# Two chained nets on one core: the passage between them by token halves

## The chip, the core and the metric

The kernel runs on one core of a Trainium2 chip. The core has five engines with queues of their own: TensorE (PE in the profile, its weight loads PEld), VectorE (DVE), ScalarE (ACT), GpSimd (POOL) and SyncE (SP), from whose queue most transfers are issued. The metric is the device time of one execution in microseconds.

## The reference, cut to what matters

Input x has 512 tokens of 1024 channels. The first net has two layers (attention mixers and a gated feed-forward net); behind them stands an RMS norm with gain `g_final`. Its result goes into the second net, again two layers. What lies around the passage is this:

```
# end of the first net, layer 1
x = x + (silu(h @ w1) * (h @ w3)) @ w2
x = rms_norm(x, g_final)
# start of the second net, layer 0
shift, scale, gate = split(c @ w_ada + b_ada, 3)
h = layer_norm(x) * (1 + scale) + shift
proj = h @ w_in        # q, k, v, gates, convolution, Fourier part
...
x = layer_norm(ALPHA * x + (1 + gate) * y) * ln_g + ln_b
```

## The kernel before, in words

Activations lie transposed: a tile is 128 channels by 512 tokens, and x is eight such tiles. Matrix products are done as three products each of a high and a low part (lines 269 to 271, `mm3`); weights are loaded by `weights` (L263), and split into `whi` on ScalarE (L251) and `wlo` on VectorE (L252). There are two staging buffers `wst` and three pairs `whi`, `wlo`. PSUM has eight banks: three with the tag "mm", two "S", two "T", one "O"; a tag that doesn't exist, such as "ms", takes a "T".

**The last products of the first net.** The loop over n in `first_layer` makes one output tile per round: 22 steps of three products over `gh`, `gl` with the `w2` weights in three parts of 8, 8 and 6 steps. The function `f` in `build` (L1647) adds the residual `xo`, and `centre` follows: it squares the tile, forms `d = g * x - shift` (L1134, the tile `u`), squares that, and sends `d` by two transfers (L1137) to `hl[:, n]` and to `xd`. For tiles 1 to 6 GpSimd adds the three tiles to running sums. At n = 6 three products with a matrix of ones (`add_sum`, L1114) put those running sums into three banks; at n = 7 three more add the last tile, the modulation's gate is folded (L1103), and mean and scale of the norms are worked out on ScalarE and VectorE for all 512 tokens, with a root (L1185) and a reciprocal (L1194).

**The modulated input.** `less_mean` subtracts the mean (L1201 for tiles 3, 5, 7 on GpSimd, L1205 for the others on VectorE), and `put_h` makes the product with the scale (L1275), the high part `hh` on ScalarE (L1276) and the low part `hl` on VectorE (L1279). The subtractions on VectorE are let go one by one with `issue_after`, and the products use the tile tag `tmp` with four buffers. After that stands the reciprocal for `r0` (L1234).

**The value products.** `second_layer` first makes values and the Fourier input: four weight chunks `wvf2`, each for two tiles k of h, against four token tiles of 128: for each chunk, each k and each token tile three products of 384 columns. The splits of chunks 2 and 3 are put behind the third tile's product and high part (`self.behind`). Then come the key projection (24 products of 512 columns, tile `mm<-hh,whi`) and the rest of the layer.

**What sets the order.** The kernel is written as one program; a planner (`TileContext` with a simulated time line) orders each engine's queue: at every moment it gives the engine, of the instructions that are ready by its own estimates, the one that stands first in the program. `issue_after` adds an order on one engine and nothing else. Semaphores are put in by the planner. The tile pools are a stack: the feed-forward pools `ft1` and `fg1` (with `gh` and `gl`) are closed at the end of the first net, and the second net's pools `t2` and `c2` are opened in their memory; `xt`, the tiles with the mean taken off, are the first of `t2`.

Of the kernel before, what the change touches and what calls it, by code (L numbers as in the profile page):

```python
# [11 lines left out]
F32 = mybir.dt.float32  # L12
# [7 lines left out]
D = 1024  # L20
# [11 lines left out]
COFF = (0, -8, -16)  # L32
RPW = 64

GATES = (1, 0, 6, 1, 1, 4, 3)
W1 = 1.0
PAUSE = (12000, 9000)
# [177 lines left out]
class _Net:  # L215
# [357 lines left out]
    def first_layer(self, l, acc, xsrc, emit_x):  # L573
# [121 lines left out]
        with ExitStack() as fctx:  # L695
            self.tp = fctx.enter_context(self.tc.tile_pool(name=f"ft{l}", bufs=4))
            gp = fctx.enter_context(self.tc.tile_pool(name=f"fg{l}", bufs=1))
            r = gp.tile([P, S], F32, name=f"rf{l}")
            gh = gp.tile([P, NF, S], F32R, name=f"gh{l}")
            gl = gp.tile([P, NF, S], F32R, name=f"gl{l}")  # L700
            h = (self.hh, self.hl)
            extra = self.modulation() if l == DEPTH - 1 else iter(())
            for i in range(NF):
                for _ in range(3):
                    next(extra, None)
                pa, pb = self.any_bank(), self.any_bank()
                self.dense(pa, self.weights(a["w1"][l, i]), h, range(8))
                if i == 0:
                    self.inv_root(self.ones_sum(acc2), D, self.eps, r)
                self.dense(pb, self.weights(a["w3"][l, i]), h, range(8))  # L710
                u = self.t(self.tp, "u", (P, S), bufs=2)
                nc.vector.tensor_tensor(u, pa, r, op=ALU.mult)
                s = self.t(self.tp, "s", (P, S), bufs=2)
                nc.scalar.activation(s, u, AF.Silu)  # L714
                nc.gpsimd.tensor_tensor(s, s, r, op=ALU.mult)  # L715
                nc.vector.tensor_tensor(u, pb, s, op=ALU.mult)
                self.split(gh[:, i], gl[:, i], u)
            for n in range(8):
                ps = self.any_bank()
                for c0 in range(0, NF, 8):  # L720
                    c1 = min(c0 + 8, NF)
                    self.dense(ps, self.weights(a["w2"][l, n][:, c0 * P:c1 * P]), (gh, gl), range(c0, c1),
                               first=c0 == 0, last=c1 == NF)
                xo = self.t(self.tp, "xo", (P, S), bufs=2)
                nc.sync.dma_start(out=xo, in_=self.xd[2 * l][n])
                emit_x(n, ps, xo)
# [389 lines left out]
    def centre(self, n, x, state):  # L1116

        nc = self.nc
        g = self.col("g_final", n)
        if n == 0:  # L1120
            z = self.t(self.tp, "tmp", (P, S))
            nc.scalar.activation(z, x, AF.Copy, scale=g)
            pz = self.bank("ms")
            self.add_sum(pz, z, True, True)
            self.shift = self.fp.tile([P, S], F32, name="shift", tag="accf")
            nc.scalar.activation(self.shift, pz, AF.Copy, scale=1.0 / P)
            state["d"], state["x"] = (self.t(self.tp, "mw", (P, S), bufs=2) for _ in range(2))
            state["q"] = self.t(self.tp, "q", (P, S), bufs=1)
            d, sq, dq = state["d"], state["x"], state["q"]
        else:  # L1130
            d = self.t(self.tp, "u", (P, S), bufs=2)
            sq, dq = (self.t(self.tp, "tmp", (P, S)) for _ in range(2))
        nc.scalar.activation(sq, x, AF.Square)
        nc.vector.scalar_tensor_tensor(d, x, g, self.shift, op0=ALU.mult, op1=ALU.subtract)  # L1134
        nc.scalar.activation(dq, d, AF.Square)
        for dst in (self.hl[:, n].bitcast(F32), self.xd[0][n]):
            nc.sync.dma_start(out=dst, in_=d)  # L1137
        if 0 < n < 7:
            for k, y in (("d", d), ("x", sq), ("q", dq)):
                nc.gpsimd.tensor_tensor(state[k], state[k], y, op=ALU.add)  # L1140
        if n == 6:
            self.pm, self.pv, self.px = (self.bank(t) for t in "SOT")
            self.add_sum(self.px, state["x"], True, False)
            self.add_sum(self.pm, state["d"], True, False)
            self.add_sum(self.pv, state["q"], True, False)
            self.root_table(sq)
        if n == 7:
            self.add_sum(self.px, sq, False, True)
            self.add_sum(self.pm, d, False, True)
            at = self.add_sum(self.pv, dq, False, True)  # L1150
            pg = self.bank("mm")
            with self.tc.issue_after(at.ins):
                self.fold(pg, [self.gate_acc])

            self.mean = self.fp.tile([P, S], F32, name="mean", tag="accf")
            m2, q = (self.t(self.tp, t, (P, S), bufs=2) for t in ("s", "xo"))
            r = self.scale = self.fp.tile([P, S], F32, name="scale")
            nc.scalar.activation(m2, self.pm, AF.Square, scale=1.0 / D)
            nc.scalar.activation(self.mean, self.pm, AF.Copy, scale=1.0 / D)
            nc.vector.tensor_scalar(q, self.px, 1.0 / D, EPS, op0=ALU.mult, op1=ALU.add)  # L1160
            nc.vector.scalar_tensor_tensor(m2, q, LN_EPS, m2, op0=ALU.mult, op1=ALU.subtract)
            self.root_of(r, self.pv, m2, ALU.add, 0.0)
            self.one_over(r, r)
            with self.tc.issue_after(self.r_at):
                self.put_mod(0, pg, 2, 1)

    def root_table(self, x):

# [25 lines left out]
        self.r_at = self.nc.vector.reciprocal(r, v).ins  # L1194
        return r

    def less_mean(self, out, x, m, use):

        nc, late = self.nc, self.tc.issue_after
        for n in (3, 5, 7):  # L1200
            nc.gpsimd.tensor_tensor(out[n], x[n], m, op=ALU.subtract)  # L1201

        def sub(n, at):
            with late(at):
                nc.vector.tensor_tensor(out[n], x[n], m, op=ALU.subtract)  # L1205

        sub(0, self.v_at)
        for n in range(8):
            at = use(n)
            if n == 0:  # L1210
                sub(1, at)
            if n + 2 in (2, 4, 6):
                sub(n + 2, at)

    def silu2(self, ps, out):

        t = self.t(self.tp, "tmp", (P, S))
# [3 lines left out]
    def second_net(self):  # L1221
        nc, a, tc = self.nc, self.a, self.tc
        with ExitStack() as ctx:
# [1 line left out]
            self.tp = pool("t2", 4)  # L1225
            cp = self.cp = pool("c2")
            self.obufs, self.roww = 2, P
            xt = [x[:, i] for x in [self.t(self.tp, "p" + t, (P, 2, S), bufs=2) for t in "hhll"] for i in range(2)]
            self.less_mean(xt, [self.hl[:, n].bitcast(F32) for n in range(8)], self.mean,
                           lambda n: self.put_h(0, n, xt[n], self.scale))  # L1230
            self.r0 = cp.tile([P, S], F32, name="r0")
            sd = self.t(self.tp, "tmp", (P, S))
            nc.scalar.activation(sd, self.px, AF.Sqrt, scale=1.0 / D, bias=self.eps)
            nc.vector.reciprocal(self.r0, sd)  # L1234
            chan = cp.tile([P, 2, P], F32, name="chan")
            nc.sync.dma_start(out=chan, in_=a["chan"][0:2].rearrange("i p n -> p i n"))
# [45 lines left out]
    def second_layer(self, l, cp, chan, ind, ropex):  # L1282
# [11 lines left out]

        v2 = self.t(cp, "v2", (P, 4, 2, P), F32R)
        fh, fl = self.t(cp, "f2h", (P, 4, 256), F32R), self.t(cp, "f2l", (P, 4, 256), F32R)
        banks = [self.bank(x) for x in "SSOT"]
        for c in range(4):
            with ExitStack() as late:
                for i in self.behind if c > 1 else ():  # L1300
                    late.enter_context(self.tc.issue_after(i))
                w = self.weights(a["wvf2"][l, c])
            for i in range(2):
                k = 2 * c + i
                for tk in range(4):
                    sl = slice(tk * P, (tk + 1) * P)
                    self.mm3(banks[tk][:, 0:384], self.hh[:, k, sl], self.hl[:, k, sl], w[0][:, i * 384:(i + 1) * 384],
                             w[1][:, i * 384:(i + 1) * 384], k == 0, k == 7)
        for tk in range(4):
            self.split(v2[:, tk, :, 0:64], v2[:, tk, :, 64:128], banks[tk][:, 0:P].rearrange("p (h d) -> p h d", h=2))  # L1310
            self.split(fh[:, tk], fl[:, tk], banks[tk][:, P:384])
# [281 lines left out]
    def build(self):  # L1593
        nc, a, tc = self.nc, self.a, self.tc
        with ExitStack() as ctx:
# [46 lines left out]
            def emit(l):  # L1642
                state = {"acc": None}

                def f(n, ps, xo):
                    xn = self.t(self.tp, "xn", (P, S), bufs=2)
                    nc.vector.tensor_tensor(xn, ps, xo, op=ALU.add)  # L1647
                    self.tap(f"xf{l}", xn, n * P)
                    if l + 1 < DEPTH:
                        nc.sync.dma_start(out=self.xd[2 * l + 1][n], in_=xn)  # L1650
                        self.to_h(n, xn, self.col(f"g_mix{l + 1}", n))
                    if l == DEPTH - 1:
                        self.centre(n, xn, state)
                        return
                    if n == 7:
                        self.acc = cst.tile([P, S], F32, name=f"acce{l}", tag="accf")
                    state["acc"] = self.add_square(state["acc"], xn, self.acc if n == 7 else None)
# [24 lines left out]
```

## Time and profile before

| | |
|---|---|
| median of 3 runs | 2393.24 us (2392.01 to 2393.78) |
| the profiled execution | 2390.04 us |
| its span | 2388.3 us |
| TensorE busy | 2312.2 us, 97% |
| VectorE busy | 1581.2 us, 66% |
| ScalarE busy | 1171.2 us, 49% |
| GpSimd busy | 708.5 us, 30% |
| mean granted TensorE clock | 0.988 |

The profile is of one execution. A timeline's row has the start, the length, the engine, the line and the operation, what it writes and reads (out<-in), how many of it stand in the row, and in brackets how long the engine was idle before and what released it. Lengths of neighbours overlap; the distance of two starts is what one costs. The passage lies between 1831 and 1886 us.

### The profile page before, as it was taken

The numbers are of one execution on the slowest core, as the hardware profiler recorded it, in microseconds if no ns is written. First come the engines' busy times: TensorE is split into PE (matmuls) and PEld (weight loads), VectorE is DVE, ScalarE is ACT, GpSimd is POOL, SyncE is SP. The second block draws the span as 40 slices with busy tenths as digits, with TensorE's granted clock in tenths as the row PEclk, the third lists the DMA queues.
The fourth block names the chain that finished last, engine by engine and source line by source line (L and its number), as shares of the span: only waits on it lengthen the run. The fifth ranks groups of instructions, "written<-read, shape, count | busy, mean of one in ns | idle before, by whom it ended". The sixth has DMA issues, their size and how long they took to land. (4 is left out here: it accounts for less than half of the span.)

```text
span 2388.3 us, 31708 instructions
## 1 busy us (share of the span) xinstructions
PE 2312.2 (97%) x11356; PEld 1927.4 (81%) x11356; DVE 1581.2 (66%) x2367; ACT 1171.2 (49%) x2064; POOL 708.5 (30%) x773
## 2 busy tenths in 40 slices
PE   8999999999999999999999999999999899979995
PEld 7888887888888888888887888878877788758884
DVE  6878797775444334878698775876333876686766
ACT  5666685544222223666685544323222465346653
POOL 3225456332111001225366332111111221332215
PEclk9999999999999999999999999999999999989998
DMA  5455557564333344465466666875343432323222
GB/s 188 145 159 168 148 168 225 190 199 159 98 97 97 100 132 143 149 184 140 146 168 208 200 197 208 274 248 175 95 147 122 126 94 80 96 90 103 85 76 79
DMA packets 129709, 352.58 MB, mean 148 GB/s; under 512 B 20856, under 2 KB 28248, under 8 KB 129552
## 3 DMA queue, kind: packets, MB, share of 16 engines
q1 hardware_dynamic: 103760, 279.91, 36.8%
q0 software_dynamic: 25792, 70.65, 10.4%
q8 instruction: 89, 1.46, 0.2%
q14 instruction: 68, 0.56, 0.1%
HBM read 281.54 MB, written 41.66 MB: 135 GB/s over the span
## 5 line engine op out<-in xcount | busy, mean ns | idle before, releaser
L251 ACT ACTIVATE whi<-wst 128x1024 fp32r<-128x1024 f32 (+4 forms) x387 | 374.1, 967 | 581.3 <-PE mm L270 160.3
L252 DVE TENSOR_TENSOR wlo<-wst,whi 128x1024 fp32r<-128x1024 f32 (+4 forms) x387 | 485.4, 1255 | 255.7 <-ACT whi L251 254.8
L269 PE MATMUL mm<-hh,whi 128*128 128x512 f32 x1184 | 471.8, 399 | 0.0
L271 PE MATMUL mm<-hh,wlo 128*128 128x512 f32 x1184 | 466.9, 394 | 0.8 <-DVE wlo L252 0.7
L270 PE MATMUL mm<-hl,whi 128*128 128x512 f32 x1184 | 466.3, 394 | 0.0
L271 PEld LDWEIGHTS mm<-hh,wlo 128*128 128x128 f32 x1184 | 223.1, 188 | 48.6 <-DVE wlo L252 1.7
L270 PEld LDWEIGHTS mm<-hl,whi 128*128 128x128 f32 x1184 | 223.8, 189 | 40.1 <-issue 0.2
L269 PEld LDWEIGHTS mm<-hh,whi 128*128 128x128 f32 x1184 | 223.5, 189 | 40.4 <-issue 0.2
L715 POOL TENSOR_TENSOR s<-s,rf 128x512 f32<-128x512 f32 x44 | 75.8, 1723 | 399.2 <-ACT s L714 399.2
L365 PE MATMUL T<-ident,E 128*128 128x128 f32 x768 | 118.4, 274 | 7.1 <-ACT E L350 6.2
L541 POOL DMA_DIRECT2D ry<-tmp x136 | 68.1, 506 | 183.5 <-ACT tmp L538 113.6
L417 POOL TENSOR_TENSOR O<-O,ll 64x256 f32<-64x256 f32 x72 | 78.6, 1096 | 138.4 <-DVE O L416 132.2
L251 ACT ACTIVATE ph<-T 128x512 fp32r<-128x512 f32 x160 | 94.9, 597 | 48.6 <-PE T L365 46.5
L365 PEld LDWEIGHTS T<-ident,E 128*128 128x128 f32 x768 | 94.2, 141 | 25.4 <-ACT E L350 7.0
L341 PE MATMUL S<-qk,qk 128*128 128x512 f32 (+2 forms) x512 | 106.2, 324 | 0.0
L252 DVE TENSOR_TENSOR pl<-T,ph 128x512 fp32r<-128x512 f32 x128 | 87.4, 684 | 28.0 <-ACT ph L251 27.5
L350 ACT ACTIVATE E<-E,stats 128x256 f32<-128x256 f32 (+1 forms) x160 | 73.0, 457 | 58.4 <-DVE stats L348 57.8
L303 POOL TENSOR_TENSOR tmp<-tmp,tmp 128x512 f32<-128x512 f32 x26 | 41.9, 1612 | 170.8 <-ACT tmp L299 166.8
L269 PE MATMUL S<-hh,whi 128*128 128x512 f32 x208 | 82.3, 396 | 5.4 <-ACT hh L254 5.4
L341 PEld LDWEIGHTS S<-qk,qk 128*128 128x128 f32 x512 | 79.5, 189 | 9.6 <-issue 0.3
L271 PE MATMUL S<-hh,wlo 128*128 128x512 f32 x208 | 82.0, 394 | 1.6 <-DVE wlo L252 1.6
L270 PE MATMUL S<-hl,whi 128*128 128x512 f32 x208 | 82.2, 395 | 0.0
(649 smaller groups left out, 5486.3 us busy)
## 6 DMA issues: line engine op xcount, KB each, us to landing
wst<-win SPq DMA_DIRECT2D x153, 512.0 KB, 4.1
wst<-w SPq DMA_DIRECT2D x120, 512.0 KB, 3.6
mw<-wada SPq DMA_DIRECT2D x48, 512.0 KB, 4.4
td<-gate SPq DMA_DIRECT2D x48, 256.0 KB, 3.3
qk<-qk POOLq DMA_DIRECT2D x40, 256.0 KB, 4.5
ry<-tmp POOLq DMA_DIRECT2D x136, 64.0 KB, 3.9
V<-vd POOLq DMA_DIRECT2D x16, 512.0 KB, 5.7
wst<-wo SPq DMA_DIRECT2D x16, 512.0 KB, 3.5
```

What stands on the lines that cost most here:

```text
L251: nc.scalar.activation(hi, src, AF.Copy)
L252: nc.vector.tensor_tensor(lo, src, hi.bitcast(F32), op=ALU.subtract)
L269: mm(out, ah, bh, start=start, stop=False, **kw)
L270: mm(out, ah, bl, start=False, stop=False, **kw)
L271: mm(out, al, bh, start=False, stop=stop, **kw)
L303: self.nc.gpsimd.tensor_tensor(new, acc, sq, op=ALU.add)
L341: nc.tensor.matmul(sp[:, i * nk:(i + 1) * nk], a, b, start=n == 0, stop=n == len(ops) - 1)
L350: nc.scalar.activation(e[:, sl], e[:, sl], AF.Exp, scale=-1.0, bias=m, accum_out=d)
L365: nc.tensor.transpose(tp[:, i * P:(i + 1) * P], e[:, i * P:(i + 1) * P], self.ident)
L417: self.summed = nc.gpsimd.tensor_tensor(dst, dst, lo, op=ALU.add)
L541: nc.gpsimd.dma_start(out=y[r:r + 32], in_=f[r ^ 32:(r ^ 32) + 32])
L715: nc.gpsimd.tensor_tensor(s, s, r, op=ALU.mult)
```

## The change

The last output tile (layer 1, n = 7) is made in two halves of 256 tokens, each in a bank of its own, with all three weight parts held. `centre_last` takes the place of the n = 7 part of `centre` and works half by half through sums, mean, scale and reciprocal; the sums of tiles 0 to 6 go into six half banks. `enter` takes the place of `less_mean` and `put_h` there: for each half tiles 0 to 5, then tiles 6 and 7 whole, with the product written over the subtraction's tile. The value products of layer 0 go in rounds: chunks 0 to 2 for token tiles 0 and 1, the same chunks for token tiles 2 and 3, then chunk 3 for all.

```diff
+HALVES = (slice(0, S // 2), slice(S // 2, S))
...
+                if l == DEPTH - 1 and n == 7:
...
+                    ws = [self.weights(a["w2"][l, n][:, c0 * P:c1 * P]) for c0, c1 in parts]
+                    pss = []
+                    for c in HALVES:
+                        pss.append(self.bank("mm")[:, c])
+                        for w, (c0, c1) in zip(ws, parts):
+                            self.dense(pss[-1], w, (gh[:, :, c], gl[:, :, c]), range(c0, c1), first=c0 == 0, last=c1 == NF)
+                    emit_x(n, pss, xo)
+                    break
...
-            self.pm, self.pv, self.px = (self.bank(t) for t in "SOT")
...
+            self.pm, self.pv, self.px = ([self.bank(t)[:, c] for t, c in zip(x, HALVES)] for x in (("S", "S"), ("O", "mm"), ("T", "T")))
...
+    def centre_last(self, ps, xo, xn):
...
+        for i, c in enumerate(HALVES):
+            nc.vector.tensor_tensor(xn[:, c], ps[i], xo[:, c], op=ALU.add)
+            nc.scalar.activation(sq[:, c], xn[:, c], AF.Square)
+            nc.vector.scalar_tensor_tensor(d[:, c], xn[:, c], self.col("g_final", n), self.shift[:, c], op0=ALU.mult,
+                                           op1=ALU.subtract)
+            nc.scalar.activation(dq[:, c], d[:, c], AF.Square)
+            px, pm, pv = self.px[i], self.pm[i], self.pv[i]
+            self.add_sum(px, sq[:, c], False, True)
+            self.add_sum(pm, d[:, c], False, True)
+            at = self.add_sum(pv, dq[:, c], False, True)
...
+            self.root_of(r[:, c], pv, m2[:, c], ALU.add, 0.0)
+            self.one_over(r[:, c], r[:, c])
+        for dst in (self.hl[:, n].bitcast(F32), self.xd[0][n]):
+            nc.sync.dma_start(out=dst, in_=d)
...
+    def enter(self):
...
+        def put(n, c):
+            shift = mod[:, 0, n:n + 1]
+            hi, lo = self.hh[:, n, c], self.hl[:, n, c]
+            x = xt[n][:, c]
+            (nc.gpsimd if n in (3, 5, 7) else nc.vector).tensor_tensor(x, lo.bitcast(F32), self.mean[:, c], op=ALU.subtract)
+            at = nc.vector.scalar_tensor_tensor(x, x, mod[:, 0, 8 + n:9 + n], self.scale[:, c], op0=ALU.mult, op1=ALU.mult)
+            put = nc.scalar.activation(hi, x, AF.Identity, bias=shift)
+            nc.vector.scalar_tensor_tensor(lo, x, shift, hi.bitcast(F32), op0=ALU.add, op1=ALU.subtract)
+            return at.ins, put.ins
+
+        for c in HALVES:
+            for n in range(6):
+                behind = put(n, c)
+                if n == 2 and c is HALVES[0]:
+                    self.behind = behind
+        for n in (6, 7):
+            put(n, slice(0, S))
...
-            self.less_mean(xt, [self.hl[:, n].bitcast(F32) for n in range(8)], self.mean,
-                           lambda n: self.put_h(0, n, xt[n], self.scale))
+            self.enter()
...
-            nc.scalar.activation(sd, self.px, AF.Sqrt, scale=1.0 / D, bias=self.eps)
+            for x, c in zip(self.px, HALVES):
+                nc.scalar.activation(sd[:, c], x, AF.Sqrt, scale=1.0 / D, bias=self.eps)
...
+        if l == 0:
+            banks = [self.bank(x) for x in ("O", "S", "S", "T")]
+            rounds = [((0, 1, 2), (0, 1)), ((0, 1, 2), (2, 3)), ((3,), (0, 1, 2, 3))]
+        else:
+            banks = [self.bank(x) for x in "SSOT"]
+            rounds = [((c,), range(4)) for c in range(4)]
+        ws = {}
+        for cs, tks in rounds:
+            for c in cs:
+                with ExitStack() as late:
+                    for i in self.behind if c > 1 and c not in ws else ():
+                        late.enter_context(self.tc.issue_after(i))
+                    w = ws[c] = ws.get(c) or self.weights(a["wvf2"][l, c])
```

## Rows read from the trace of the kernel before

**Rows 1.** The page's first part: busy time, share of the span, instructions of each engine.

```profile
PE 2312.2 (97%) x11356; PEld 1927.4 (81%) x11356; DVE 1581.2 (66%) x2367; ACT 1171.2 (49%) x2064; POOL 708.5 (30%) x773
```

**Rows 2.** TensorE's waits from 1849 to 1960 us: total, times, longest.

```profile
PE S L269 <- ACT hh L1276: 6.3, 1, 6.3
PE T L1114 <- ACT tmp L1133: 1.4, 1, 1.4
```

**Rows 3.** Timeline of TensorE: start, length, instruction, idle time before.

```profile
1831.10 0.39 PE L269 MATMUL mm<-gh,whi 128*128 128x512 f32 x1
1838.56 1.02 PE L1114 MATMUL T<-mw,onef 128*128 128x512 f32 x2
1848.82 0.39 PE L271 MATMUL mm<-gh,wlo 128*128 128x512 f32 x1
1853.40 1.84 PE L1103 MATMUL mm<-onef,macc 128*128 128x1 f32 x16
1861.79 0.69 PE L269 MATMUL S<-whi,hh 128*128 128x384 f32 x1 [6.32 <-ACT hh L1276]
...
1863.24 0.52 PE L269 MATMUL O<-whi,hh 128*128 128x384 f32 x1
1863.56 0.52 PE L270 MATMUL O<-wlo,hh 128*128 128x384 f32 x1
...
1870.16 0.33 PE L270 MATMUL S<-wlo,hh 128*128 128x384 f32 x1
1870.33 0.33 PE L269 MATMUL O<-whi,hh 128*128 128x384 f32 x1
...
1885.60 0.40 PE L271 MATMUL mm<-hh,wlo 128*128 128x512 f32 x1
```

**Rows 4.** Timelines of VectorE, GpSimd and SyncE's queue across the passage.

```profile
1850.04 0.75 DVE L1134 SCALAR_TENSOR_TENSOR u<-xn,cols,shift 128x512 f32<-128x512 f32 x1
...
1855.93 0.17 DVE L1362 MEMSET fm<- 128x128 f32 x1 [1.06 <-DMA xd<-u]
1856.65 3.35 DVE L1194 RECIPROCAL scale<-scale 128x512 f32<-128x512 f32 x1
1867.82 0.95 DVE L252 TENSOR_TENSOR wlo<-wst,whi 128x768 fp32r<-128x768 f32 x1
1873.53 3.35 DVE L1234 RECIPROCAL r<-tmp 128x512 f32<-128x512 f32 x1
...
1855.91 1.85 POOL L1201 TENSOR_TENSOR ph<-hl,mean 128x512 f32<-128x512 f32 x1 [18.52 <-DMA xd<-u]
...
1851.33 0.59 SPq L1137 DMA_DIRECT2D xd<-u  x1
```

**Rows 5.** Prices of half-wide work: groups by form; timelines of VectorE and TensorE.

```profile
L1194 DVE RECIPROCAL mu<-rs 128x256 f32<-128x256 f32 x2 | 3.5, 1739 | 0.0
1880.83 0.76 DVE L252 TENSOR_TENSOR dft0l<-tmp,dft0h 128x258 fp32r<-128x258 f32 x2
94.82 0.28 PE L271 MATMUL mm<-whi,hl 128*128 128x256 f32 x1
94.94 0.28 PE L269 MATMUL mm<-whi,hh 128*128 128x256 f32 x1
```

**Rows 6.** Timelines of VectorE and GpSimd where both read half-wide tiles.

```profile
2373.92 0.94 DVE L1535 TENSOR_TENSOR dft0l<-dft0l,mu 128x256 f32<-128x256 f32 x1
2374.79 0.75 DVE L1535 TENSOR_TENSOR dft1h<-dft1h,mu 128x256 f32<-128x256 f32 x2
...
2372.75 0.96 POOL L1533 TENSOR_TENSOR dft0l<-dft0l,mu 128x256 f32<-128x256 f32 x1 [3.61 <-DVE mu L1194]
```

**Rows 7.** Windows: busy time of the engines, granted clock, DMA share, GB/s.

```profile
1861.70:1871.00 9.30, 9.21 (x44) 9.21 (x45) 9.30 (x15) 5.35 (x9) 0.00 (x0) 0.82 0.13 29
```

**Rows 8.** Timeline of VectorE in the second net's own passage between layers.

```profile
2138.77 3.34 DVE L1194 RECIPROCAL r<-rs 128x512 f32<-128x512 f32 x1
...
2142.60 0.95 DVE L252 TENSOR_TENSOR wlo<-wst,whi 128x768 fp32r<-128x768 f32 x1
```

More of the change, by code (lines that the diff above doesn't have):

```diff
@@ L718, in first_layer @@
             for n in range(8):
+                if l == DEPTH - 1 and n == 7:
+                    xo = self.t(self.tp, "xo", (P, S), bufs=2)
+                    nc.sync.dma_start(out=xo, in_=self.xd[2 * l][n])
+                    parts = [(c0, min(c0 + 8, NF)) for c0 in range(0, NF, 8)]
+                    ws = [self.weights(a["w2"][l, n][:, c0 * P:c1 * P]) for c0, c1 in parts]
[6 more added lines that the diff above has]
+                    break
                 ps = self.any_bank()
@@ L1141, in centre @@
         if n == 6:
-            self.pm, self.pv, self.px = (self.bank(t) for t in "SOT")
-            self.add_sum(self.px, state["x"], True, False)
-            self.add_sum(self.pm, state["d"], True, False)
-            self.add_sum(self.pv, state["q"], True, False)
-            self.root_table(sq)
[L1147 to L1165, printed above, removed]
@@ new lines, in centre @@
+            self.pm, self.pv, self.px = ([self.bank(t)[:, c] for t, c in zip(x, HALVES)] for x in (("S", "S"), ("O", "mm"), ("T", "T")))
+            for i, c in enumerate(HALVES):
+                self.add_sum(self.px[i], state["x"][:, c], True, False)
+                self.add_sum(self.pm[i], state["d"][:, c], True, False)
+                self.add_sum(self.pv[i], state["q"][:, c], True, False)
+            self.root_table(sq)
+    def centre_last(self, ps, xo, xn):
+        nc, n = self.nc, 7
+        d = self.t(self.tp, "u", (P, S), bufs=2)
+        sq, dq = (self.t(self.tp, "tmp", (P, S)) for _ in range(2))
+        pg = self.bank("mm")
+        self.mean = self.fp.tile([P, S], F32, name="mean", tag="accf")
+        m2, q = (self.t(self.tp, t, (P, S), bufs=2) for t in ("s", "xo"))
+        r = self.scale = self.fp.tile([P, S], F32, name="scale")
+        for i, c in enumerate(HALVES):
+            nc.vector.tensor_tensor(xn[:, c], ps[i], xo[:, c], op=ALU.add)
[7 more added lines that the diff above has]
+            at = self.add_sum(pv, dq[:, c], False, True)
+            nc.scalar.activation(m2[:, c], pm, AF.Square, scale=1.0 / D)
+            nc.scalar.activation(self.mean[:, c], pm, AF.Copy, scale=1.0 / D)
+            nc.vector.tensor_scalar(q[:, c], px, 1.0 / D, EPS, op0=ALU.mult, op1=ALU.add)
+            nc.vector.scalar_tensor_tensor(m2[:, c], q[:, c], LN_EPS, m2[:, c], op0=ALU.mult, op1=ALU.subtract)
+            self.root_of(r[:, c], pv, m2[:, c], ALU.add, 0.0)
+            self.one_over(r[:, c], r[:, c])
+        for dst in (self.hl[:, n].bitcast(F32), self.xd[0][n]):
+            nc.sync.dma_start(out=dst, in_=d)
+        with self.tc.issue_after(at.ins):
+            self.fold(pg, [self.gate_acc])
+        with self.tc.issue_after(self.r_at):
+            self.put_mod(0, pg, 2, 1)
@@ new lines, in enter @@
+    def enter(self):
+        nc, mod = self.nc, self.mod
+        xt = [x[:, i] for x in [self.t(self.tp, "p" + t, (P, 2, S), bufs=2) for t in "hhll"] for i in range(2)]
+        def put(n, c):
[14 more added lines that the diff above has]
+            put(n, slice(0, S))
@@ L1195, in one_over @@
         return r
[L1197 to L1213, printed above, removed]
     def silu2(self, ps, out):
@@ L1227, in second_net @@
             self.obufs, self.roww = 2, P
-            xt = [x[:, i] for x in [self.t(self.tp, "p" + t, (P, 2, S), bufs=2) for t in "hhll"] for i in range(2)]
-            self.less_mean(xt, [self.hl[:, n].bitcast(F32) for n in range(8)], self.mean,
-                           lambda n: self.put_h(0, n, xt[n], self.scale))
+            self.enter()
             self.r0 = cp.tile([P, S], F32, name="r0")
             sd = self.t(self.tp, "tmp", (P, S))
-            nc.scalar.activation(sd, self.px, AF.Sqrt, scale=1.0 / D, bias=self.eps)
+            for x, c in zip(self.px, HALVES):
+                nc.scalar.activation(sd[:, c], x, AF.Sqrt, scale=1.0 / D, bias=self.eps)
             nc.vector.reciprocal(self.r0, sd)
@@ L1296, in second_layer @@
         fh, fl = self.t(cp, "f2h", (P, 4, 256), F32R), self.t(cp, "f2l", (P, 4, 256), F32R)
[L1297 to L1308, printed above, removed]
+        if l == 0:
[11 more added lines that the diff above has]
+                    w = ws[c] = ws.get(c) or self.weights(a["wvf2"][l, c])
+                for i in range(2):
+                    k = 2 * c + i
+                    for tk in tks:
+                        sl = slice(tk * P, (tk + 1) * P)
+                        self.mm3(banks[tk][:, 0:384], self.hh[:, k, sl], self.hl[:, k, sl], w[0][:, i * 384:(i + 1) * 384],
+                                 w[1][:, i * 384:(i + 1) * 384], k == 0, k == 7)
         for tk in range(4):
@@ L1646, in f @@
                     xn = self.t(self.tp, "xn", (P, S), bufs=2)
+                    if isinstance(ps, list):
+                        self.centre_last(ps, xo, xn)
+                        return
                     nc.vector.tensor_tensor(xn, ps, xo, op=ALU.add)
```

## The prediction

> **What bounds the kernel now.** I read the page's first part first: TensorE is busy 97% of the span [rows 1], so the time falls only where TensorE is idle or slowed. Its waits around the passage come next: from 1849 to 1960 us it waits 6.3 us for the first tile of the modulated input and 1.4 us for the square of the last output tile, and but for 0.3 us nothing else [rows 2]. Its timeline gives the order: the last output tile's products run from 1831.10 to 1849.2, the sums and the modulation's fold end about 1855.2, and the first value product comes at 1861.79 after 6.32 us of idleness [rows 3]. From there TensorE is never idle up to the last step of the key projection, 1885.6 + 0.4 = 1886.0. So the passage can give back at most 7.7 us of waiting, and a clock loss: value products lie 0.32 us apart at 1863 and 0.17 at 1870 [rows 3], and the granted clock of that stretch is 0.82, a mix of the levels 1.2 and 2.4 GHz [rows 7]. The loss is 24.2 us (1861.79 to 1886.0) less 96 value products at 0.173, 24 projection steps at 0.23 and 0.14 for a small one, 22.3 together: 1.9 us.
>
> Then VectorE and GpSimd, which set that order. GpSimd's first subtraction starts at 1855.91, released by the copy of `u` to `xd`, which it does not read; VectorE's memset of `fm` at 1855.93 waited for the same copy [rows 4]. I read this as: the second net's tile pool, which takes the memory of the feed-forward pool, opens only when the last user of that whole pool is done. VectorE then works nearly without a break (9.30 of 9.30 us [rows 7]).
>
> **The change part by part.** All against the profiled execution, 2390.04 us (span 2388.3); the median of the runs shown is 2393.24, 3.2 above it, and I add the same difference to it.
>
> *Last output tile in halves.* 66 steps become 132. Half-wide steps lie 0.12 apart [rows 5]; a whole step takes 0.23 (17.72 us from 1831.10 to 1848.82, less some 2.6 for the three sums, by 65 [rows 3]). 15.8 against 15.4: +0.4, so the end is 1849.6. Six half sums for three whole ones: nothing. All three weight parts must be there for the first half, and the next layer's first two can be split only during the second half; both fit, since a split takes 0.95 us of VectorE, idle there.
>
> *First half's sums and norm.* The planner gives each engine, of what is ready, what stands first in the program; the sums of tile 6 cut into tile 7's products at 1838.56 [rows 3] because they stand before them. The first half's last sums stand behind both halves' products, so they run after 1849.6: only its sum, squares and difference are hidden.
>
> *Opening of the pool.* Before: `u` starts at 1850.04, its second copy is issued at 1851.33, the pool opens at 1855.91, 5.9 us after `u` starts [rows 4]. After: `u` of the second half starts at 1849.6 + 0.4. Opening at 1855.8; bounds 1855.4 (by `u`) and 1856.7 (another weight transfer now falls into the same burst). So the first half's modulated input cannot start under the second half's products, whatever its norm says.
>
> *Norm.* Two reciprocals of 1.74 [rows 5] for one of 3.35. They run before the opening, ending near 1856.3, instead of 1856.65 to 1859.95. A subtraction, a product and the rounding, half wide, then give the first value product at about 1858.0: 3.8 us earlier.
>
> *VectorE after the opening; here the gain goes.* A half-wide two-tile operation advances by 0.34 (a pair takes 0.76 [rows 5]); I take 0.365 as a mean with the three-operand ones. First half: 4 subtractions, 6 products, 6 remainders; second half the same; 32 × 0.365 = 11.7. Tile 6 whole: 1.9. The old code held the subtractions back with `issue_after` and had four `tmp` buffers, so VectorE ran out of higher work at times, and the split of weight chunk 2 got in at 1867.82 [rows 4]. In the new code all subtractions and products of both halves are ready from the start, and they stand before the weight split in the program, as does the reciprocal for `r0` (3.35 [rows 4]). In the second net's own passage, the same order is seen: the reciprocal of `r` at 2138.77 goes ahead of a weight split at 2142.60 [rows 8]. So the split of chunk 2 falls behind nearly all of it, and first products of both halves stop at k = 4. While GpSimd subtracts, VectorE is slower: 0.94 for one half-wide operation beside a GpSimd one of 0.96, where two alone take 0.75, so one 0.41 [rows 6]; four such cost 4 × 0.53, a whole one about twice that, 3.2; one lies beside the reciprocal, 2.7 left. Before, these lay beside the 3.35 us reciprocal [rows 4]. Sum: 1856.3 + 11.3 (one pair waits longer) + 1.9 + 3.35 + 2.7 + 0.95 = 1876.5 for the end of chunk 2's split. Bounds: 1862 (split right behind the third tile) and 1880 (all of tile 7 ahead, too).
>
> By the Trainium skill (SBUF — State Buffer, section Who interferes with whom) the shared port pair goes as a whole to whichever of a VectorE operation with two inputs in SBUF and a GpSimd operation starts first, and the other fully blocks. By that rule VectorE could stand through all of GpSimd's four half and one whole operation; at 0.96 each and 1.9 that would be 5.7 in place of 2.7.
>
> *TensorE after it.* By then it has done k = 0 to 3 of both halves and four single products of k = 4, 52 of 96. 44 × 0.173 = 7.6, the key projection 24 × 0.23 = 5.5, 0.14, and the clock: idle for some 7 us before 1876.5, longer than the idleness that led to 0.82, so 1.9 again (bounds 0 and 3.8). 1876.5 + 15.1 = 1891.6 against 1886.0: **+5.6 us**, less 0.3 for small sums of the gains' constants that now fill idle time. From there TensorE is the bound on both sides. Forecast +5.3: 2395.3 for the profiled execution, **2398.5** as median. By the skill's rule 3.0 more, 2401.5.
>
> **Rivals.** (A) *Not slower: the split gets in early.* If the planner finds VectorE free after the third tile (`behind` names it), nothing stops TensorE from 1858.0 on, and the 3.8 us stay, less 0.5 to 1 for VectorE's extra instructions: −3, 2390.2. For it: chunk 2's split did get in among the products before [rows 4]. Against: what let it in is taken away.
> (B) *Full overlap.* If the opening goes by address, not by pool, the first half's inputs are ready at 1849.6 and only the second half's norm shows: 6.3 of waiting and 1.9 of clock saved, +0.4 paid, less 0.5 for other work: about −8, 2385. Against: GpSimd's release in [rows 4].
> (C) *Slower by less.* The reciprocal of `r0` falls behind the split: 3.35 less, +2, 2395.2. It needs TensorE's and ScalarE's idle slots to place `r0` later than I think; [rows 8] speak against it.
> (D) *VectorE loses more to GpSimd,* as one whole operation of GpSimd's for each of its own: +3.0 on the forecast, 2401.5. The first GpSimd subtraction, 1.85 [rows 4], speaks for it, the measured 0.94 against. This is what the skill's rule above would make of it.
>
> **How the numbers follow.** Forecast 0.45, A 0.22, B 0.10, C 0.15, D 0.08. 0.2% is 4.8 us, about what this measurement can tell from no change. The forecast alone runs from 2395 to 2401 and lies above +4.8 six times in ten (0.27 of slower), D gives 0.08, C 0.03: slower 0.38. B and a quarter of A, with a little for a later stage that happens to run better: faster 0.19. Same 0.43. The range runs from 2387 (it leaves out B and the best of A) to 2402 (it leaves out the worst of D).
>
> **What would show it.** In the profile after: GpSimd's and VectorE's first subtraction at the same 1855.5 to 1856.7, released by the copy of `u`; the first value product near 1858; a second wait of TensorE of 5 to 9 us inside the value products, released by VectorE's `wlo` of the weight split; that split behind a 3.35 us reciprocal to `r0`; the key projection ending near 1891.5; granted clock of some 0.5 around 1870 to 1878. Wrong if the split's wait is under 2 us (A), if a subtraction of the first half starts before 1853 (B), or if the key projection ends before 1886.

## The result: 16.9 us slower

After: 2410.43 us (median of 4 runs, 2409.22 to 2411.69), before in the same comparison 2393.51. The ratio is 1.0069, 95% interval 1.0058 to 1.0081. The forecast was +5.3 us: the sign was right, the size a third, and the time lies above the range.

The page's first part of the kernel after, beside [rows 1]:

```profile
PE 2319.3 (96%) x11434; PEld 1935.1 (80%) x11434; DVE 1583.2 (66%) x2389; ACT 1174.6 (49%) x2076; POOL 709.6 (29%) x775
```

TensorE has 7.1 us more of busy time, for 21.6 us more of span (2409.9 against 2388.3). Its waits from 1820 to 1910 us (total, times, longest), the answer to [rows 2]:

```profile
PE O L270 <- ACT hh L1207: 10.2, 1, 10.2
PE T L1279 <- ACT tmp L1266: 4.9, 1, 4.9
PE T L1128 <- POOL mw L1154: 2.9, 1, 2.9
PE O L272 <- DVE hl L1208: 1.6, 1, 1.6
PE S L270 <- ACT hh L1207: 1.4, 1, 1.4
```

Five waits, 21 us, stand where there were 6.3 and 1.4. TensorE's timeline, the answer to [rows 3]:

```profile
1834.52 2.07 PE L1128 MATMUL T<-mw,onef 128*128 128x256 f32 x4 [2.91 <-POOL mw L1154]
1836.47 2.08 PE L1128 MATMUL S<-mw,onef 128*128 128x256 f32 x4
...
1839.20 1.06 PE L1128 MATMUL mm<-q,onef 128*128 128x256 f32 x2
1839.70 0.78 PE L270 MATMUL mm<-gh,whi 128*128 128x256 f32 x1
...
1855.66 0.28 PE L272 MATMUL mm<-gh,wlo 128*128 128x256 f32 x1
1855.78 0.60 PE L1128 MATMUL T<-tmp,onef 128*128 128x256 f32 x2
...
1865.23 0.61 PE L1279 MATMUL T<-cols,onef 128*128 128x16 f32 x2 [4.85 <-ACT tmp L1266]
1876.09 0.69 PE L270 MATMUL O<-whi,hh 128*128 128x384 f32 x1 [10.24 <-ACT hh L1207]
...
1879.61 0.52 PE L271 MATMUL S<-wlo,hh 128*128 128x384 f32 x1
1881.70 0.69 PE L272 MATMUL O<-whi,hl 128*128 128x384 f32 x1 [1.57 <-DVE hl L1208]
```

The sums of tiles 0 to 6 no longer cut into the last tile's products; they stand ahead of all of them, and TensorE waits for GpSimd's last addition. Then comes the entry (the modulated input and the first value products): one value product at 1876.09, six by 1881.7, and from there no wait until the key projection ends at 1905.1 (before: 1886.0). VectorE, GpSimd and SyncE's queue, the answer to [rows 4]:

```profile
1856.76 0.48 DVE L1176 SCALAR_TENSOR_TENSOR u<-xn,cols,shift 128x256 f32<-128x256 f32 x1
1859.43 3.35 DVE L1246 RECIPROCAL scale<-scale 128x256 f32<-128x256 f32 x2
1864.72 2.15 DVE L1205 TENSOR_TENSOR ph<-hl,mean 128x256 f32<-128x256 f32 x3 [1.92 <-DMA xd<-u]
1866.80 0.94 DVE L1205 TENSOR_TENSOR pl<-hl,mean 128x256 f32<-128x256 f32 x1
1867.66 2.68 DVE L1205 TENSOR_TENSOR ph<-hl,mean 128x256 f32<-128x256 f32 x3
1870.26 1.01 DVE L1205 TENSOR_TENSOR pl<-hl,mean 128x256 f32<-128x256 f32 x2
1871.35 0.47 DVE L1206 SCALAR_TENSOR_TENSOR pl<-pl,mod,scale 128x256 f32<-128x256 f32 x1
1871.75 3.34 DVE L1267 RECIPROCAL r<-tmp 128x512 f32<-128x512 f32 x1
1875.03 1.65 DVE L1206 SCALAR_TENSOR_TENSOR ph<-ph,mod,scale 128x256 f32<-128x256 f32 x4
...
1881.18 1.26 DVE L1208 SCALAR_TENSOR_TENSOR hl<-ph,mod,hh 128x256 fp32r<-128x256 f32 x3
1882.71 0.94 DVE L253 TENSOR_TENSOR wlo<-wst,whi 128x768 fp32r<-128x768 f32 x1
```

```profile
1864.76 0.97 POOL L1205 TENSOR_TENSOR pl<-hl,mean 128x256 f32<-128x256 f32 x1 [27.11 <-DMA xd<-u]
```

```profile
1857.02 0.43 SPq L1296 DMA_DIRECT2D ropex<-ropeX  x1
1857.49 0.48 SPq L1190 DMA_DIRECT2D hl<-u  x1
1858.01 0.59 SPq L1190 DMA_DIRECT2D xd<-u  x1
```

Both engines again start with the landing of `u`'s copy, at 1864.7. VectorE then does nine subtractions (eight half wide and, in the last row of two, tile 6 whole), one product, `r0`'s reciprocal and nearly all products, and only then remainders. A value product needs its tile's remainder third, so TensorE starts for good at 1881.70. Windows of the kernel after, as in [rows 7] (the columns that count here are PE's busy time and, behind POOL, the granted clock):

```profile
1830.00:1840.00 10.00, 7.09 (x20) 4.98 (x19) 3.36 (x3) 3.59 (x5) 3.76 (x3) 0.69 0.41 133
1860.00:1870.00 10.00, 0.99 (x6) 0.80 (x5) 8.08 (x10) 1.98 (x5) 4.96 (x5) 0.56 0.45 139
1870.00:1880.00 10.00, 2.52 (x6) 1.64 (x6) 10.00 (x22) 4.98 (x12) 0.00 (x0) 0.50 0.07 17
```

0.50 is the level of 1.2 GHz. The sums at 1834.52, right behind the wait of 2.91, are slow as well: 2.07 us for four, where two take 0.60 at 1855.78.

### The profile page after: what moved, and what is told of

The parts are those of the page before. It is cut to its first block, busy times and chain, and to the rows that moved or that the text cites. A ratio compares the mean times of both kernels' runs of the same rounds, so it can differ in the third digit from the quotient of the medians.

```text
span 2409.9 us, 31891 instructions
## 1 busy us (share of the span) xinstructions
PE 2319.3 (96%) x11434; PEld 1935.1 (80%) x11434; DVE 1583.2 (66%) x2389; ACT 1174.6 (49%) x2076; POOL 709.6 (29%) x775
## 3 DMA queue, kind: packets, MB, share of 16 engines
q1 hardware_dynamic: 103760, 279.91, 36.8%
q0 software_dynamic: 25792, 70.65, 10.3%
## 5 line engine op out<-in xcount | busy, mean ns | idle before, releaser
L270 PEld LDWEIGHTS mm<-hh,whi 128*128 128x128 f32 x1184 | 223.7, 189 | 41.9 <-ACT whi L252 1.0
L351 ACT ACTIVATE E<-E,stats 128x256 f32<-128x256 f32 (+1 forms) x160 | 72.9, 457 | 56.3 <-DVE stats L349 55.6
```

What stands on the lines that cost most here:

```text
L270: mm(out, ah, bh, start=start, stop=False, **kw)
L351: nc.scalar.activation(e[:, sl], e[:, sl], AF.Exp, scale=-1.0, bias=m, accum_out=d)
```

## The experiments

Four sets were run, each beside the kernel before; its median moved between 2391.3 and 2395.4 over the sets, so kernels are compared by their ratio to it (0.001 is 2.4 us). The passage is measured in each trace, as intervals, in us: *tile 7* from the end of tile 6's products to the end of tile 7's; from there *to the first value product* and *to the key projection's end*; *idle* is TensorE's idle time from tile 7's end to the key projection's. *Passage* is tile 7 and the key projection's end together.

| kernel | ratio, 95% interval | tile 7 | to first product | to key end | passage | idle |
|---|---|---|---|---|---|---|
| before | 1 | 18.0 | 12.6 | 36.8 | 54.7 | 7.7 |
| after | 1.0069, 1.0058 to 1.0081 | 24.3 | 20.1 | 49.1 | 73.5 | 18.1 |
| sums_between | 1.0048, 1.0036 to 1.0061 | 18.0 | 20.0 | 49.6 | 67.6 | 17.9 |
| r0_last | 1.0063, 1.0050 to 1.0075 | 24.9 | 17.0 | 47.2 | 72.1 | 15.7 |
| old_entry | 1.0069, 1.0056 to 1.0081 | 25.2 | 13.7 | 47.6 | 72.9 | 14.4 |
| new_entry | 1.0056, 1.0042 to 1.0070 | 18.0 | 22.0 | 51.9 | 69.9 | 20.6 |
| vec_subs | 1.0064, 1.0050 to 1.0078 | 23.0 | 13.6 | 46.5 | 69.5 | 14.6 |
| own_pool | 1.0079, 1.0066 to 1.0092 | 23.0 | 8.6 | 48.4 | 71.4 | 14.0 |
| old_entry_sums | 1.0041, 1.0029 to 1.0053 | 18.0 | 13.8 | 47.5 | 65.5 | 14.9 |
| full_overlap | 1.0012, 1.0003 to 1.0021 | 21.1 | 0.2 | 36.7 | 57.8 | 6.6 |
| one_bank | 1.0071, 1.0056 to 1.0085 | 25.3 | 15.7 | 46.8 | 72.2 | 16.4 |
| old_entry_one_bank | 1.0011, 1.0002 to 1.0020 | 17.1 | 10.9 | 36.5 | 53.6 | 5.3 |
| own_pool_one_bank | 0.9998, 0.9989 to 1.0007 | 17.1 | 9.6 | 37.8 | 54.9 | 5.5 |
| full_overlap_2 | 1.0006, 0.9996 to 1.0016 | 19.3 | 0.4 | 32.2 | 51.5 | 4.8 |
| sums_one_bank | 1.0041, 1.0027 to 1.0055 | 17.1 | 14.5 | 45.9 | 63.1 | 14.5 |
| own_pool_sums | 1.0047, 1.0034 to 1.0059 | 18.0 | 8.6 | 47.7 | 65.7 | 14.0 |

**One part at a time.** *sums_between*: the six sums of tile 6 stand between the last tile's halves.

```diff
                             self.dense(pss[-1], w, ...)
+                        if c is HALVES[0]:
+                            self.sums_of_six()
```

> The changed kernel, but the six half sums of tiles 0 to 6 stand between the two halves of the last output tile instead of ahead of it. Theory (the losses lie one behind the other): TensorE's wait of 2.9 us for GpSimd's sum at 1834.5 goes, the sums run at the full clock (2.6 us in place of 5.2), the last tile ends near 1849.7 instead of 1855.8, and all that follows moves with it: 5.5 to 6.3 us less than the changed kernel, some 2404.5. Rival 1 (what follows is held by transfers and by VectorE's order, not by the tile's end): less than 3 us. Rival 2 (the weight transfer that collides with the copies of u moves out of their way too): about 8 us, the pool opening 6 us after u and not 8.

Tile 7 takes 18.0 us again and the ratio falls by 0.0021, 5.0 us, a little less than expected and within the intervals: the theory holds, and the rest of the passage changes by under 0.5 us.

*r0_last*: `r0`'s reciprocal waits for the last remainder.

```diff
+            with tc.issue_after(self.last_put):
+                nc.vector.reciprocal(self.r0, sd)
```

> The changed kernel, but the reciprocal for r0 (3.34 us) is held behind the last remainder of the modulated input. Theory (it stands on the path to the first value product): that product comes at 1872.7 instead of 1876.1, and 3 to 4 us are saved, some 2407. Rival (VectorE has the same sum of work ahead of the key projection whatever the order, and the wait only moves to the remainders or to the split of chunk 2): within 1 us of the changed kernel, 2410.

The first product comes 3.1 us earlier behind the tile, the key projection's end 1.9: part of it is lost again, 0.7 us at small sums of the gains' constants (the tile `rq`). 1.4 us by the ratio, inside the intervals; the rival is nearer.

*old_entry*: halves for the last tile and the norm only; subtractions, products and value rounds as before.

```diff
-            self.enter()
+            self.less_mean(xt, [...], self.mean, lambda n: self.put_h(0, n, xt[n], self.scale))
```

> The last output tile, its sums and its norm in halves as in the changed kernel, but the modulated input and the value products as in the kernel before (less_mean, put_h, whole tiles, chunks in turn). Theory (some 6 us are lost ahead of the tile's end, 2 at the pool's opening, the rest in the new order of VectorE): 2401 to 2403, the first value product 6 us after the opening. Rival (the new entry costs nothing by itself, all is lost in the last tile and its norm): 2409 to 2411.

No gain: the theory fell. The first value product comes 4.9 us after the opening (1867.49 to 1872.39), not 11.4, and 6.5 us earlier behind the tile than in the kernel after, but TensorE stops again:

```profile
1890.63 0.56 PE L1311 MATMUL T<-rq,onef 128*128 128x8 f32 x2 [5.01 <-ACT dft0h L252]
```

```profile
1883.99 3.34 DVE L1287 RECIPROCAL r<-tmp 128x512 f32<-128x512 f32 x1
...
1890.32 0.16 DVE L1309 TENSOR_TENSOR rq<-bcol 128x8 f32<-128x8 f32 x1
```

These are the sums of the gains' constants, with a fixed place in TensorE's order; they read `rq`, which VectorE ends at 1890.48, and the release that the profile names is not what they read. Their bank, T, has two buffers, and both are held by `px`, now two half-filled banks, until `r0`'s root has read them. Behind that stands a chain on VectorE (`gbar`, `bcol`, `rq`), queued behind `r0`'s reciprocal. Before, `px` held one buffer, and these sums ran in idle time, at 1855.10. That was a new theory: two banks for `px` cost what the early start brings.

*new_entry* is the other part alone, on the kernel before: whole last tile, `enter` and the rounds in halves.

```diff
-            self.less_mean(...)
+            self.enter()
```

> The kernel before, but with the modulated input by halves (enter) and the value products in rounds; last output tile, sums and norm whole as before. Theory: VectorE has subtractions, the reciprocal for r0 and some splits ahead of the first product, the first value product comes 7 to 9 us later than before (1861.8), part of it is caught up: 2399 to 2404. Together with the run that has only the other part, the two differences from the kernel before add up to about the 17 us of the change. Rival (the entry alone is neutral): within 2 us of the kernel before, 2391.5 to 2395.5.

13 us of loss (0.0056) without any of the rest, more than expected: VectorE's order alone puts the first product 22.0 us behind the tile. Either part alone costs nearly the whole, and the two do not add up to the change's 17 as expected, so the costs hide one another and can't be read by taking one away.

**The theory's pieces.** *vec_subs*: all subtractions on VectorE.

```diff
-            (nc.gpsimd if n in (3, 5, 7) else nc.vector).tensor_tensor(x, lo.bitcast(F32), ...)
+            nc.vector.tensor_tensor(x, lo.bitcast(F32), ...)
```

> The changed kernel, but all subtractions on VectorE, none on GpSimd. In the order of its instructions the reciprocal for r0 then stands behind the products, not ahead of them. Theory (TensorE is held by the first remainder, third in its fixed order): thirteen subtractions in 4.6 us against nine in 6.5 beside GpSimd; the first value product comes 6 us after the opening, not 11.4, but the first remainder some 14 after it against 16.5; 2 to 3 us less than the changed kernel, 2407 to 2408.5. Rival (the first product decides): 5 to 6 us less, 2404.5. Rival 2 (GpSimd's help is worth having): slower, above 2411.

In the trace the tile's end to the key projection's is 2.7 us shorter, 0.9 of it by an earlier opening (7.0 us after `u`, not 8.0); the ratio does not tell it from the kernel after.

*own_pool*: the half-wide tiles stand in buffers that are free before the late pool opens.

```diff
-            x = xt[n][:, c]
+            x = self.t(self.tp, "half", (P, S // 2), bufs=9)
```

> The changed kernel, but the modulated input's intermediate tiles lie in the feed-forward stage's own pool (nine half-wide tiles), so they don't wait for the second net's pool to open; tiles 6 and 7 by halves, too. Sums of tiles 0 to 6 still ahead of the last tile. Theory (the wait for the pool, and with it nine subtractions beside GpSimd and the reciprocal for r0 ahead of the products, is what delays the value products; the early subtractions now lie under the norm): first value product 7 to 8 us after the last tile's end, not 20; the key projection ends 8 to 16 us earlier; 2394 to 2402. Rival (the pool only sets the start, VectorE's sum of work sets the end): 3 us or less, above 2407.

The theory fell: 11.5 us earlier at the first product, 0.8 at the key projection's end, and no gain by the ratio (tiles 6 and 7 go by halves here, too). *old_entry_sums* is old_entry with the edit of sums_between:

> Last output tile and norm in halves, sums of tiles 0 to 6 between the halves, entry and value products as before the change. In the run with the old entry and the sums ahead, the loss was 18 us from tile 6's end to the key projection's: 8 of it by the sums, 2 by the opening, 5 in a wait of TensorE for the gains' constants, whose bank is freed by the root for r0. Theory (these add up): 5 to 6 us less than that run, 2405 to 2407. Rival (without the early sums the constants' sum and the key weights fall into place as before): 2396 to 2400.

6.7 us less than old_entry by the ratios; the wait for `rq` stays, 5.05 us.

*full_overlap*: as own_pool, and each half's sums, norm and entry as soon as its products are done, so that value products of the first half run beside the second half's sums.

```diff
+                            if i == 1 and c0 == 0:
+                                emit_x(n, (0, pss[0]), xo)
...
+                        if i == 0:
+                            self.sums_of_six()
+                    emit_x(n, (1, pss[1]), xo)
```

> All together: tiles in the feed-forward stage's pool, the sums of tiles 0 to 6 between the two halves, the first half's sums and norm written among the second half's products, the last tile's difference read where it is made, the reciprocal for r0 behind the split of the values. Theory (full overlap was possible, the pool and the orders stood against it): value products of the first half follow the second half's last product without a gap over 1 us; a gap of 2 to 5 us before those of the second half; 6 to 9 us below the kernel before, 2385 to 2389. Rival 1 (VectorE has too much work between the two: the gap only moves): within 3 us of the kernel before. Rival 2 (the second half's norm waits behind the first half's modulation on VectorE and ScalarE): 2396 to 2402.

TensorE goes on 0.2 us after the tile, yet the time is 0.0012, 2.9 us, above the kernel before: TensorE then waits 6.4 us, 2.8 of them for `rq`, and the second half's norm, 11.6 us long on VectorE (1855.8 to 1867.4), stands behind the first half's remainders and a split.

**The bank.** `px` in one bank; its second half is started only when its first is summed.

```diff
-            self.pm, self.pv, self.px = (... (("S", "S"), ("O", "mm"), ("T", "T")))
+            self.pm, self.pv = (... (("S", "S"), ("O", "mm")))
+            px = self.bank("T")
+            self.px = [px[:, c] for c in HALVES]
...
+            self.add_sum(px, self.six[0][:, c], True, False)
             self.add_sum(px, sq[:, c], False, True)
```

*one_bank* is that alone on the kernel after; *old_entry_one_bank* the same on old_entry_sums.

> The kernel after, but both halves of the residual's sums (px) stand in one bank, so that the second bank of the name T is free for the constants' sums of the first value products and queries. Theory (in the kernel after the start is set by the first remainder of VectorE, and the waits for that bank lie inside time in which TensorE idles anyway): no more than 1.5 us off the kernel after, 2408 to 2411. Rival (the held bank costs here what it cost in the kernel with the old entry, some 5 us): 2403 to 2406.

> The old entry behind the sums in halves (old_entry_sums), with both halves of px in one bank. Theory (the 5 us for which TensorE stands at the constants' sums of the queries come from the bank that px holds, and nothing else is late behind it): 5 to 7 us below old_entry_sums, so 2396 to 2400, within 6 us of the kernel before; no wait over 1 us for a buffer of T. Rival (VectorE's or the key weights' work is late at the same place anyway): 2401 to 2404, with a wait of the same length under another name.

The theory holds in both. In the kernel after the 4.85 us lie in idle time and the ratio stays. With the old entry it falls by 0.0030, 7.2 us, and no wait for T is left; the key projection's steps also go among the value products again, from 25.8 us behind the tile instead of 41.9. Not all of the 7.2 need be the bank's: in this kernel the planner also issues another transfer, `ropex`, behind `u`'s copies, and the first subtraction comes 5.9 us after `u`, not 8.1 (last section). The two were not separated.

*own_pool_one_bank*: own_pool, sums_between and the bank.

> The half-wide tiles in buffers that are free early (own_pool), with the six sums of tile 6 between the halves of tile 7 and px in one bank. Theory (own_pool lost its earlier start again at the constants' sums, and 5 us at the sums ahead of the last tile): 2413 less 5 less 5, so 2400 to 2405, key projection's end some 60 us after the end of tile 6. Rival (VectorE is the bound, and the wait comes back for a split or a remainder): 2406 to 2411.

Better than either: 0.9998, where I had given the bank 5 us. The square of bank and buffers, with the sums mended in all four, shows why. *sums_one_bank* keeps the late pool, *own_pool_sums* the two banks.

> The kernel after with the six sums of tile 6 between the halves of tile 7 and both halves of px in one bank; the half-wide tiles still in the pool that opens late. Theory (the bank counts only where the entry does not wait for that pool): 5 us for the sums and 1 to 2 for the bank below the kernel after, so 2403 to 2406, key projection's end some 66 us after the end of tile 6, and VectorE's products and remainders still what TensorE waits for. Rival (the bank is worth here what it was beside the early buffers, 10 us and more): 2394 to 2398.

> The half-wide tiles in buffers that are free early and the six sums of tile 6 between the halves, but px's halves in two banks. Theory (sums 5 to 6 us below own_pool, and the waits for the constants' sums, some 10 us in all, stay): 2407 to 2409, key projection's end 65 us after the end of tile 6. Rival (the sums in the wrong place were what held the bank so long, and the waits go with them): 2394 to 2399.

Ratios 1.0048 with neither (sums_between), 1.0041 with the bank, 1.0047 with the early buffers, 0.9998 with both. One cure alone is worth 1.7 and 0.2 us, within the intervals; both 12. (In both kernels with the bank `ropex` stands behind the copies, too.) TensorE's waits, first with the bank alone, then with the buffers alone, then with both:

```profile
PE O L270 <- ACT hh L1215: 8.9, 1, 8.9
PE O L272 <- DVE hl L1216: 5.6, 1, 5.6
```

```profile
PE T L1294 <- DVE rq L1292: 4.9, 1, 4.9
PE O L270 <- ACT hh L1210: 4.2, 1, 4.2
PE S L272 <- DVE hl L1211: 2.2, 1, 2.2
PE O L272 <- DVE hl L1211: 1.9, 1, 1.9
PE T L1282 <- ACT tmp L1269: 0.8, 1, 0.8
```

```profile
PE T L1297 <- DVE rq L1295: 3.4, 1, 3.4
PE S L272 <- DVE hl L1214: 1.3, 1, 1.3
PE O L272 <- DVE hl L1214: 0.6, 1, 0.6
PE O L270 <- ACT hh L1213: 0.3, 1, 0.3
```

With the bank alone TensorE waits for the entry, 14.5 us in all. With the buffers alone it starts early and stands at `rq`. VectorE and TensorE of own_pool_sums there:

```profile
1875.16 3.35 DVE L1270 RECIPROCAL r<-tmp 128x512 f32<-128x512 f32 x1 [0.76 <-ACT tmp L1269]
1878.43 0.11 DVE L1284 TENSOR_REDUCE gbar<-T 128x2 f32<-128x16 f32 x1
...
1880.01 0.16 DVE L1292 TENSOR_TENSOR rq<-bcol 128x8 f32<-128x8 f32 x1
```

```profile
1880.31 0.56 PE L1294 MATMUL T<-rq,onef 128*128 128x8 f32 x2 [4.89 <-DVE rq L1292]
```

The chain from `gbar` to `rq` needs the bank that `px` gives up, and so stands behind `r0`. With one bank the first of these sums runs beside the last tile's, and the second, with its 3.4 us, ahead of the value products:

```profile
1851.40 0.29 PE L1285 MATMUL T<-cols,onef 128*128 128x16 f32 x2
...
1858.55 0.57 PE L1297 MATMUL T<-rq,onef 128*128 128x8 f32 x2 [3.36 <-DVE rq L1295]
1859.40 0.69 PE L270 MATMUL O<-whi,hh 128*128 128x384 f32 x1 [0.28 <-ACT hh L1213]
```

*full_overlap_2*: full_overlap with the bank, the first half's sums right behind its products, and VectorE's order held by `issue_after`.

```diff
+                if c is HALVES[1] and n not in (3, 5, 7):
+                    late.enter_context(self.tc.issue_after(self.m_at if n else self.v_at))
```

> Full overlap of the first half's entry with the second half's sums, with px in one bank, the first half's sums right behind its products, and VectorE's order by what the second half's norm needs: the second half's subtractions behind the first half's scalings, the splits of chunks 1 and 2 behind the products that need VectorE first, one root for both halves. Theory (what kept full_overlap at the time of the kernel before was the second half's norm chain at the tail of VectorE's queue, 11.6 us long, and the bank of the constants' sums): 2385 to 2391, faster than the kernel before by 3 to 9 us. Rival (VectorE has as much work in all and only shifts the wait): 2396 to 2400, as full_overlap.

The passage is the shortest of all, 51.5 us against 54.7, but the time is that of the kernel before. What follows the key projection takes 508.6 us in this trace against 502.3; of the difference 3.8 are waits of TensorE (23.9 in all against 20.1). Single traces differ there by several us (502.3 to 508.6), and the profiled execution of before lies 4.4 below the median of 29 runs. Whether the 3 us are lost later or were never there is not settled.

## Why the prediction was wrong

**What bounds the kernel, and the opening's mechanism: right.** The pool opens with the landing of `u`'s copy. *"Opening at 1855.8"*, 5.9 us after `u`, was 8.0 after it: the copy took 6.6 us from issue to landing against 4.4. 2.1 us, where the forecast's bound for another weight transfer in the same burst allowed 0.9.

***"Six half sums for three whole ones: nothing"* failed**: 6.3 us. I took their place from the program's order in [rows 3]; the planner put them first in TensorE's fixed order, where they wait 2.91 us for GpSimd and then run slowly, in a stretch of a granted 0.69 (5.2 us from 1834.52 to 1839.70; 2.6 in the sum for before). sums_between gave 5.0 back. Why the planner put them there was not tried.

***"A subtraction, a product and the rounding, half wide, then give the first value product"* is the step that failed most.** It names the shortest chain, not VectorE's order: all nine subtractions and `r0`'s reciprocal, which I had put ahead of the weight split, go ahead of the first half's products, too. Measured: 11.4 us from the opening to the first value product (1864.72 to 1876.09) where I took 2.2. In the program a tile's product stands ahead of the next tile's subtraction, so the program's order alone does not give this; what in the planner's estimates does was not looked into.

***"By then it has done [...] 52 of 96"* failed** for the same reason: 6 when TensorE starts for good. VectorE's amount was about right: the chunk-2 split ends 18.9 us after the opening, forecast 20.7. But no split was what TensorE waited for: the third product of each tile waited for its remainder, behind all subtractions, `r0` and nearly all products. Behind 1881.70 TensorE had 90 value products left, 23.4 us to the end; I took 15.1 behind the split.

**The reciprocal of `r0` ahead of the split and two reciprocals ahead of the opening: right. The granted clock near 0.5 at 1870 to 1878: right by luck**, since the idle time stood ahead of the value products and not, as forecast, among them behind the split. By the forecast's own sign, a wait for the split of under 2 us, its mechanism did not occur; nor did that of A, which the sign was to point to.

***"less 0.3 for small sums of the gains' constants that now fill idle time"***: true of this kernel, where 4.85 us of waiting for them lie in idle time. The forecast had no rival in which `px`'s two banks hold them back, and at them old_entry and own_pool lose 5.0 and 5.1 us of their earlier start.

**The sum of the loss**, by the ratios on the way from the kernel after to own_pool_one_bank: sums 5.0, bank 1.7, late buffers 10.3, together 17.0 us, for 16.9 by the medians. The last two are shares only in this order; the square shows that neither stands alone. old_entry_one_bank takes the last step by the old entry instead, and gives 7.2 of the 10.3.

**Rivals.** A, B and C needed an entry that starts early; full_overlap built B's: its start came, its 8 us did not. D: VectorE's nine subtractions took 6.53 us (1864.72 to 1871.25). In vec_subs, with none on GpSimd, half-wide ones follow each other at 0.335 and the whole one takes 0.60:

```profile
1863.96 1.35 DVE L1205 TENSOR_TENSOR pl<-hl,mean 128x256 f32<-128x256 f32 x3
1865.23 0.17 DVE L1124 TENSOR_SCALAR mod<-mod 128x8 f32<-128x8 f32 x1
```

So the nine alone would take 3.3, and GpSimd cost 3.2, where I took 2.7 and D 5.7. The price of the forecast was right; it had one GpSimd operation lie beside the reciprocal, and none did. By the Trainium skill (SBUF — State Buffer, Who interferes with whom) one of the two fully blocks. The trace fits turns of that kind, but at less than a full operation's price: both engines' half-wide subtractions start 0.86 us apart, more than either takes alone (VectorE 0.34, GpSimd 0.72 at 2377.61 in the kernel before) and less than the two together. D is worth 0.5 us of the 11.6 that the forecast missed.

Two sums of the prediction are off and change nothing: 1856.65 and 3.35 make 1860.00, not 1859.95, and B's terms (6.3 and 1.9 saved, 0.4 and 0.5 paid) make 7.3, not 8.

## What to carry to other kernels

A piece that is ready early is worth nothing if the engine that serves it first does the same step for all pieces: count what is ready at the opening and can come ahead of the first thing that the bound engine needs, whatever the program's order says, and do not forecast by the shortest chain. When a result is split in two, ask whether it now holds two buffers and who else takes that name. When one cure at a time brings nothing, try pairs: here two cures gave 1.7 and 0.2 us alone and 12 together.

## What the runs showed of the hardware

How long `u`'s copy took went with the transfers beside it. In the kernel before, `ropex` (512 KB) is issued ahead of `u`'s two copies, at 1850.23, and the second copy lands 4.4 us after its issue. In the kernel after, a second weight transfer stands in the same burst (issued at 1855.62, landed at 1858.69), and the copy lands after 6.6; in all nine kernels with both ahead of the copies it takes 5.3 to 6.6. In the three kernels in which the planner issues `ropex` behind the copies, with both weight transfers still ahead (sums_one_bank, old_entry_one_bank, own_pool_one_bank), it takes 3.3 to 3.6. In sums_one_bank the first subtraction then comes 5.7 us after `u` instead of 8.0:

```profile
1850.28 0.47 SPq L1198 DMA_DIRECT2D hl<-u  x1
1850.80 0.59 SPq L1198 DMA_DIRECT2D xd<-u  x1
1851.43 0.43 SPq L1304 DMA_DIRECT2D ropex<-ropeX  x1
```

In sums_between and in one_bank it still stands ahead; no edit asked for the new place, the planner gave it when both were made. No run moves `ropex` alone, so what its place is worth in time is not shown.
